# A hybrid decoder layer: the MLP's second product in seven block products as well, in quarters, with more weight sums by DMA and more small sums on GpSimd

## The chip, the cores and the metric

The kernel is one program on one NeuronCore of a Trainium2 chip. The metric is device time in microseconds (us), from one launch; the span is the time from the first to the last instruction in a profiled execution.

## The reference, cut to what matters

One decoder layer on 512 tokens of width 1024: retention and sparse attention in parallel, a merge and an output projection, then the MLP and a gate with per-layer embeddings. All is float32. The part that matters here:

```python
x = x + (g_ret * o_ret + g_nsa * o_nsa) @ w_out[i]
h2 = rms_norm(x, norm_mlp_g[i])
x = x + jnp.square(jax.nn.relu(h2 @ w_mlp_up[i])) @ w_mlp_down[i]      # 1024 -> 4096 -> 1024
x = x + (p[i] @ w_ple_proj[i]) * jax.nn.sigmoid(rms_norm(x, norm_ple_g[i]) @ w_ple_gate[i])
return rms_norm(x, norm_final_g)
```

## The kernel before, in words

Activations lie transposed: partitions are features, the 512 columns are tokens. Float32 accuracy comes from splitting each operand into a high and a low part; a product of a 128x128 weight tile with a block of activations is three matmuls (hi·hi, hi·lo, lo·hi; `mm3`, L264 to L266), summed in PSUM. Weights come by DMA into a ring of three `raw` tiles of 128x1024 (512 KB). Each half of such a tile (128x512) is split by `split_part`: ScalarE copies the high part (L214), VectorE subtracts for the low part (L217). High and low parts have rings of four.

The order of the work is a list of `Item`s that `run` goes through: for each item the splits of its weights, its matmuls, then splits for items ahead (`look`), then the deferred functions, then its `post` (what reads PSUM). Every engine executes its own instructions in the order in which this list issues them.

The MLP's first product (Up, 1024 to 4096) is done in seven block products instead of eight: tokens in two halves of 256, the contraction in two halves, the hidden outputs in pairs of 128. Per pair `UpPair` makes the products m1, m2, p3 to p7, each 4 x 3 matmuls of 256 columns. Their activations (x00, x10, x11 and the sums t1 to t4) are made once, at the end of the out projection, by `combined`, whose sums are on GpSimd (L1390 to L1392). Their weights are blocks of `w_mlp_up` and four sums of blocks, s1 to s4, which are built in DRAM earlier, during the retention heads: 32 plain copies issued from ScalarE and 32 accumulating DMAs issued from GpSimd (`sum_steps`, L360). After the products VectorE and ScalarE add the pieces, VectorE squares (L1489), ScalarE takes the high part (L1490), VectorE the low part (L1491).

The second product (Down, 4096 to 1024) is plain: per output tile 16 x 3 matmuls of 512 columns per half of the hidden width (`down`). The order is Up for the first half of the hidden width, Down for it, Up for the second half, Down for it. Then come the embedding gate (PLE), for which stored products `pp` are loaded during the last Down, the final norm and the output.

## Time and profile before

| | |
|---|---|
| three timed runs | 1250.19, 1251.27, 1254.92 us; median 1251.27 |
| the profiled execution | 1252.07 us, its span 1250.2 us |
| PE busy | 1227.0 us, 98% of the span |
| VectorE (DVE), ScalarE (ACT), GpSimd (POOL) | 67%, 46%, 19% |
| granted TensorE clock | 0.996 of full speed |

The page divides the span among engines and lines; the views behind it give single instructions in order of time, groups, waits and DMA queues. PE at 98% says that almost any time that PE is not spared is not saved; a helper engine's share says little until it is read stage by stage. Lengths of PE instructions are modelled and overlap; what one costs is read from the distance between starts.

### The profile page before, as it was taken

How to read it: one execution, taken by the hardware profiler on the slowest of the kernel's cores; microseconds unless marked ns; L12 is line 12 of the kernel's file. 1: busy time of each engine (PE TensorE's matmuls, PEld its weight loads, DVE VectorE, ACT ScalarE, POOL GpSimd, SP SyncE). 2: the span in 40 equal slices, each digit the busy share in tenths (PEclk: the TensorE clock that was granted, in tenths of full speed). 3: DMA queues.
4: the chain of work that ended last, by engine and by line, in shares of the span. 5: the costliest groups of instructions: out<-in, count | busy, mean ns of one | idle time of the engine just before them, and what ended most of it. 6: DMA issues, size and time to landing. Idle time of an engine off the chain costs nothing.

```text
span 1250.2 us, 18607 instructions
## 1 busy us (share of the span) xinstructions
PE 1227.0 (98%) x6888; PEld 1047.8 (84%) x6888; DVE 835.9 (67%) x1594; ACT 579.1 (46%) x1215; POOL 237.3 (19%) x234
## 2 busy tenths in 40 slices
PE   7999999999999999999999999999999999999996
PEld 6968898998988887788888878889998889988885
DVE  6766764666667478678878863578883348854567
ACT  5753334332333233567877752366552236633333
POOL 0050110111110014256755600012000000000033
PEclk9999999999999999999999999999999999999998
DMA  7545994887685232211110023334552335563221
GB/s 251 193 138 151 251 234 132 218 214 199 173 226 152 68 93 84 68 52 34 35 35 19 34 68 101 103 134 153 186 178 93 99 115 185 179 213 101 90 80 68
DMA packets 64458, 162.55 MB, mean 130 GB/s; under 512 B 6512, under 2 KB 6896, under 8 KB 64368
## 3 DMA queue, kind: packets, MB, share of 16 engines
q1 hardware_dynamic: 46816, 127.54, 30.9%
q0 software_dynamic: 8704, 16.78, 8.0%
q10 hardware_dynamic: 8848, 17.04, 4.1%
q8 instruction: 54, 0.88, 0.3%
q14 instruction: 36, 0.29, 0.1%
HBM read 157.15 MB, written 37.75 MB: 156 GB/s over the span
## 4 chain that ended last, share of the span: by engine, by line
PE 46%; DVE 5%; ACT 1%; issue 1%; DVEq 0%; ACTq 0%
PE ps_s L266 4%; PE ps_s L264 4%; PE ps_s L265 4%; PE ps_d L266 4%; PE ps_d L265 4%; PE ps_d L264 4%; PE ps_v L264 3%; PE ps_v L266 3%; PE ps_v L265 3%; PE ps_t L265 2%; PE ps_t L266 2%; PE ps_t L264 2%; PE ps_t L1127 2%; PE ps_v L1144 1%; PE ps_v L1143 1%; PE ps_s L1052 1%
## 5 line engine op out<-in xcount | busy, mean ns | idle before, releaser
L214 ACT ACTIVATE hi<-raw 128x512 fp32r<-128x512 f32 (+1 forms) x412 | 250.4, 622 | 238.0 <-PE ps_s L265 54.8
L217 DVE TENSOR_TENSOR lo<-raw,hi 128x512 fp32r<-128x512 f32 (+1 forms) x398 | 279.4, 717 | 58.7 <-ACT hi L214 58.4
L264 PE MATMUL ps_d<-h_hi,hi 128*128 128x512 f32 x216 | 89.6, 415 | 0.0
L266 PE MATMUL ps_d<-h_hi,lo 128*128 128x512 f32 x216 | 85.4, 395 | 0.0
L265 PE MATMUL ps_d<-h_lo,hi 128*128 128x512 f32 x216 | 85.3, 395 | 0.0
L1105 POOL TENSOR_TENSOR pr<-pr,rr 128x512 f32<-128x512 f32 x80 | 84.7, 1091 | 0.0
L217 POOL TENSOR_TENSOR lo_fw<-raw_fw,hi_fw 128x512 fp32r<-128x512 f32 x8 | 11.3, 1440 | 347.3 <-ACT hi_fw L214 347.3
L1070 ACT ACTIVATE pr<-ps_s,nm 128x128 f32<-128x128 f32 (+3 forms) x128 | 66.1, 526 | 21.2 <-DVE sc L1064 15.2
L1136 DVE TENSOR_TENSOR ptl<-ps_t,pth 128x512 fp32r<-128x512 f32 x80 | 53.9, 685 | 16.8 <-ACT pth L1131 14.8
L264 PE MATMUL ps_t<-h_hi,hi 128*128 128x512 f32 x160 | 64.1, 401 | 0.0
L266 PE MATMUL ps_t<-h_hi,lo 128*128 128x512 f32 x160 | 63.4, 396 | 0.4 <-DVE lo L217 0.4
L265 PE MATMUL ps_t<-h_lo,hi 128*128 128x512 f32 x160 | 63.3, 395 | 0.0
L1062 DVE TENSOR_REDUCE nm<-ps_s 128x2 f32<-128x256 f32 (+3 forms) x64 | 52.0, 814 | 14.3 <-PE ps_s L1055 14.0
L360 POOL DMA_DIRECT2D sum_s<-in_w_mlp_up_dram x16 | 18.3, 1147 | 222.8 <-DMA sum_s<-in_w_mlp_up_dram 222.8
L1131 ACT ACTIVATE pth<-ps_t 128x512 fp32r<-128x512 f32 x80 | 47.4, 599 | 22.2 <-PE ps_t L1127 18.3
L266 PE MATMUL ps_s<-hh,lo 128*128 128x512 f32 x128 | 50.5, 395 | 0.0
L264 PE MATMUL ps_s<-hh,hi 128*128 128x512 f32 x128 | 50.5, 395 | 0.0
L265 PE MATMUL ps_s<-hl,hi 128*128 128x512 f32 x128 | 50.5, 395 | 0.0
L266 PEld LDWEIGHTS ps_d<-h_hi,lo 128*128 128x128 f32 x216 | 40.6, 188 | 10.0 <-DVE lo L217 0.3
L1127 PEld LDWEIGHTS ps_t<-cst,pr 128*128 128x128 f32 x320 | 39.3, 140 | 10.7 <-issue 1.6
L1127 PE MATMUL ps_t<-cst,pr 128*128 128x128 f32 x320 | 48.0, 273 | 0.0
L264 PEld LDWEIGHTS ps_d<-h_hi,hi 128*128 128x128 f32 x216 | 40.7, 188 | 7.0 <-ACT tanh L433 0.4
(483 smaller groups left out, 3653.4 us busy)
## 6 DMA issues: line engine op xcount, KB each, us to landing
...
```

The source lines that it names most:

```text
L214: act.activation(p.hi[i], p.raw[:, c], AF.Copy)
L217: eng.tensor_tensor(p.lo[i], p.raw[:, c], p.hi[i].bitcast(F32), op=ALU.subtract)
L264: pe.matmul(ps, sh, mh, start=first, stop=False, skip_group_check=again)
L265: pe.matmul(ps, sh, ml, start=False, stop=False, skip_group_check=again)
L266: pe.matmul(ps, sl, mh, start=False, stop=last, skip_group_check=again)
L360: return [lambda d=d, s_=s_, add_=add_: pool.dma_start(d, s_, accum_op=ALU.add, max_dma_last_dim=4 * S) if add_ else act.dma_start(d, s_) ...
L1062: dve.tensor_reduce(self.nm[:, j, :], self.seen(j), axis=AX.XY, op=ALU.max, negate=True)
L1070: act.activation(self.pr[:, j, br, 0 : self.nk].rearrange("p (b j) -> p b j", j=P), self.seen(j)[:, br], AF.Exp, bias=self.nm[:, j, br : b ...
L1105: pool.tensor_tensor(p, p, self.rr[:, :, 1 + br : 2 + br].broadcast_to([P, 4, P]), op=ALU.mult)
L1127: pe.transpose(self.t[i][:, j * P : (j + 1) * P], self.pr[:, j, br, kb * P : (kb + 1) * P], ident)
L1131: act.activation(hi, self.t[i], AF.Copy)
L1136: dve.tensor_tensor(lo, self.t[i], self.pt[i][0].bitcast(F32), op=ALU.subtract)
```

## The change

Down gets the same seven products as Up. The hidden width goes in four quarters of 1024 instead of two halves: Up of a quarter, Down of it, and so on, eight stages of 28 products (`steps_of`, `mlp`). At each change of stage the first product of the new stage is put ahead of the last of the old one. Down's weights are laid out anew and four sums of their blocks are built like Up's: 64 copies and 64 accumulating DMAs instead of 32 and 32. Of these the first halves run in the heads as before; the other 32 copies go out from ScalarE during the attention, the other 32 accumulating DMAs from GpSimd, spread from the merge to the end of the third MLP stage. Up's results are now squared in pieces and combined per quarter into x00 to t4 (tiles `ht`): four small sums per pair on GpSimd, seven high and seven low parts of 256 columns on ScalarE and VectorE. Down's results are multiplied by the norm factor on VectorE and added to x on GpSimd (on VectorE in the last quarter). The low parts of some weights go to GpSimd: 9 of 28 in Up, 10 of 28 in Down. Two more tiles for high and low parts come from another pool, and splits go five ahead. At the end, five of nine loads for PLE are issued later, and the output tiles are others.

```diff
--- before.py
+++ after.py
@@ part_tile
+        if p.first is not None and (p.first + i) % 6 > 3:
+            return P_["ew"].tile([P, c.stop - c.start], F32R, tag=tag, name=tag, bufs=2)
         return wp.tile([P, c.stop - c.start], F32R, tag=tag, name=tag, bufs=4)
@@ run
-                    split(n)
+                    split(n, eng=pool if order[n][1] in order[n][0].other else dve)
...
-                split(j, ahead > 0)
+                split(j, ahead > 0, pool if order[j][1] in order[j][0].other else dve)
@@ sum_steps
+    wb, sums = {}, {}
+    for name in ("w_mlp_up", "w_mlp_down"):
+        wb[name] = a[name].rearrange("(q i) k (j c) -> i j q k c", i=2, j=2)
+        sums[name] = {x: dram.tile([16, P, S], F32, name=f"{x}_{name}") for x in ("s1", "s2", "s3", "s4")}
...
+            copies.append([(t["s1"], w(1, 1)), (t["s3"], w(0, 0)), (t["s2"], w(0, 0)), (t["s4"], w(0, 1))])
+            for l, level in enumerate(([("s1", w(1, 0)), ("s3", w(1, 0))], [("s2", t["s1"])], [("s4", t["s2"])])):
+                adds.setdefault(c + l, []).extend((t[x], src) for x, src in level)
+        return [[lambda x=x: act.dma_start(*x) for x in g] for g in copies], [[lambda x=x: pool.dma_start(*x, accum_op=ALU.add, max_dma_last_dim=4 * S) for x in adds[n]] for n in sorted(adds)]
@@ the list of items
-    folds_ = sum_steps()
+    chunks = [(name, 4 * qt + i) for qt in range(NQ) for name in wb for i in (0, 2)]
+    copies, adds = sum_steps(chunks[:8])
...
+    copies2, adds2 = sum_steps(chunks[8:])
...
+    copies2 = sum(copies2, [])
+    every = len(ops) // (len(copies2) + 2)
     for i, op in enumerate(ops):
+        if i % every == every - 1 and copies2:
+            add(Item(0, copies2.pop(0)))
...
+    adds2 = sum(adds2, [])
+    merge_at = len(items)
@@ class UpPair, now Pair with the subclasses Up (row0, half1, row1) and Down (added)
-            return Item(1.4, go, getattr(self, "after_" + name, None), piece.parts(col, col + S))
+            return Item(1.4, go, getattr(self, "after_" + name), piece.parts(col, col + S), 5)
...
-        def squares(self, i, t):
-            n = 2 * (self.q % 8) + i
-            hi = P_["hid"].tile([P, S], F32R, tag=f"hh{n}", name="hh")
-            lo = P_["hid"].tile([P, S], F32R, tag=f"hl{n}", name="hl")
-            dve.scalar_tensor_tensor(t, t, 0.0, t, op0=ALU.min if i else ALU.max, op1=ALU.mult)
-            act.activation(hi, t, AF.Copy)
-            defer(lambda: dve.tensor_tensor(lo, t, hi.bitcast(F32), op=ALU.subtract))
+        def row0(self):
+            k, r0 = self.q % 4, self.r0
+            d = self.d = P_["ew"].tile([P, H], F32, tag="hd", name="hd", bufs=2)
...
+            dve.scalar_tensor_tensor(r0, r0, 0.0, r0, op0=ALU.max, op1=ALU.mult)
+            pool.tensor_tensor(d, r0[:, :H], r0[:, H:], op=ALU.subtract)
+            taken("x00", k, r0[:, :H], of="ht")
+            defer(lambda: taken("t1", k, d, of="ht"))
+        def half1(self):
+            n = self.r1[:, H:]
+            dve.scalar_tensor_tensor(n, n, 0.0, n, op0=ALU.min, op1=ALU.mult)
+            taken("x11", self.q % 4, n, of="ht")
+        def row1(self):
+            k, d, r0, r1 = self.q % 4, self.d, self.r0, self.r1
+            act.activation(r1[:, :H], self.a, AF.Relu, scale=-1.0)
+            act.activation(r1[:, :H], r1[:, :H], AF.Square)
+            taken("x10", k, r1[:, :H], of="ht")
+            pool.tensor_tensor(d, d, r1[:, H:], op=ALU.add)
+            pool.tensor_tensor(r0[:, H:], r1[:, H:], r0[:, H:], op=ALU.subtract)
+            pool.tensor_tensor(r0[:, :H], d, r1[:, :H], op=ALU.subtract)
+            def rest():
+                taken("t2", k, d, -1.0, "ht")
+                taken("t3", k, r0[:, H:], of="ht")
+                taken("t4", k, r0[:, :H], of="ht")
+            defer(lambda: defer(rest))
...
+        def added(self, n, r, op):
+            dve.tensor_tensor(r, r, T["rb2"], op=ALU.mult)
+            x = T["x1"][n]
+            (pool if self.q < 12 else dve).tensor_tensor(x, x, r, op=op)
+            if self.q // 4 == NQ - 1:
+                defer(lambda: defer(lambda: gained(n, G_PLE, "acc2")))
@@ ups, down -> steps_of, mlp
-        ps_ = [Piece(a["w_mlp_down"][hf, n, c]) for c in range(2)]
-        return dense(("d", "v", "s", "s")[n % 4], ps_, (lambda: [hid[hf, i] for i in range(16)], 16), post, 4)
+        pooled = {(x, i) for x in ("m2", "p3") for i in range(4)} | ({("p7", 3)} if kind is Up else {("m1", 0), ("m1", 1)})
+        return [(qs[i], x, (x, i) in pooled) for x, i in order_]
...
+        for qt in range(NQ):
+            for kind, name in ((Up, "w_mlp_up"), (Down, "w_mlp_down")):
+                more = steps_of(kind, name, qt)
+                flat = flat[:-1] + more[:1] + flat[-1:] + more[1:] if flat else more
...
-    items += u0[:8] + [token_rstd(("acc1",), "n1", "s")] + u0[8:16] + [over_squared()] + u0[16:]
-    items += sum((down(0, n) for n in range(KT)), [])
-    items += ups(1)
-    dn = [down(1, n) for n in range(KT)]
-    items += dn[0] + [Item(0, load_pp)] + sum(dn[1:], [])
+    items += st_[0][:8] + [token_rstd(("acc1",), "n1", "s")] + st_[0][8:14] + [over_squared()] + st_[0][14:] + st_[1] + st_[2]
+    items[merge_at:] = among(items[merge_at:], adds2)
+    items += sum(st_[3:7], [])
...
+    items += [*dn[:4], Item(0, gx_start), Item(0, load_pp), *among(dn[4:], [lambda i=i: one_pp(i) for i in (0, 2, 4, 6)])]
+    late_pp = [lambda i=i: one_pp(i) for i in (1, 3, 5, 7, 8)]
...
-    items += weave(first[:16], turns[:4])
+    items += among(weave(first[:16], turns[:4]), late_pp)
...
-        "w_mlp_down": _tiles(w_mlp_down[0]).reshape(2, 2, KT, P, 1024).transpose(0, 2, 1, 3, 4),
+        "w_mlp_down": _tiles(w_mlp_down[0]).reshape(NQ * KT, P, NQ, 2, P).transpose(0, 1, 3, 2, 4).reshape(NQ * KT, P, D),
```

On VectorE, in the middle of the second Up stage, it stood like this before (`lo` is a weight's low part, `r0` and `r1` are results of a pair, `hl` the low part of the squared result, `ps` is PSUM, `s12` and `s5` saved pieces):

```order
L217 TENSOR_TENSOR lo_9704<-raw_9579,hi_9687 128x512
L217 TENSOR_TENSOR lo_9725<-raw_9623,hi_9709 128x512
L1473 TENSOR_TENSOR r0_9647<-ps_t_9463,s12_9563 128x256
L1489 SCALAR_TENSOR_TENSOR r0_9647<-r0_9647 128x512
L217 TENSOR_TENSOR lo_9747<-raw_9623,hi_9727 128x512
L1491 TENSOR_TENSOR hl_9731<-r0_9647,hh_9730 128x512
L1467 TENSOR_TENSOR r0_9754<-ps_s_9734,s12_9711 128x256
L217 TENSOR_TENSOR lo_9768<-raw_9663,hi_9751 128x512
L1478 TENSOR_TENSOR r1_9772<-ps_d_9546,s5_9480 128x256
L217 TENSOR_TENSOR lo_9786<-raw_9663,hi_9770 128x512
L217 TENSOR_TENSOR lo_9805<-raw_9706,hi_9790 128x512
L1481 COPY r1_9772<-ps_d_9546 128x256
```

After the change, on VectorE at the end of the second Up quarter (`hd` is a pair's difference, `ht` a high or low part for Down):

```order
L1518 SCALAR_TENSOR_TENSOR r0_10531<-r0_10531 128x512
L224 TENSOR_TENSOR lo_10609<-raw_10474,hi_10589 128x512
L1387 TENSOR_TENSOR ht_10179<-r0_10531,ht_10178 128x256
L1387 TENSOR_TENSOR ht_10181<-hd_10593,ht_10180 128x256
L1387 TENSOR_TENSOR ht_10171<-r1_10570,ht_10170 128x256
L1502 TENSOR_TENSOR r1_10642<-ps_v_10459,s5_10395 128x256
L1525 SCALAR_TENSOR_TENSOR r1_10642<-r1_10642 128x256
L224 TENSOR_TENSOR lo_10659<-raw_10524,hi_10638 128x512
L1387 TENSOR_TENSOR ht_10181<-r1_10642,ht_10180 128x256
L1389 SCALAR_TENSOR_TENSOR ht_10175<-hd_10505,ht_10174 128x256
L1387 TENSOR_TENSOR ht_10175<-r0_10414,ht_10174 128x256
L1387 TENSOR_TENSOR ht_10177<-r0_10414,ht_10176 128x256
```

The 512-wide low parts of results are now narrow ones, more of them, and fewer weights' low parts stand among them.

On GpSimd, from the end of the out projection on, the rows before were these, and the last of them is already in PLE (`gf`, `gd` are tiles of `combined`, `lo_fw` a gate weight's low part):

```order
L1392 TENSOR_TENSOR gf2_8408<-gd2_8411,gf_8621 128x256
L1390 TENSOR_TENSOR gd3_8460<-gd3_8460,gf_8687 128x256
L1391 TENSOR_TENSOR gf3_8457<-gf_8687,gf3_8457 128x256
L1392 TENSOR_TENSOR gf3_8457<-gd3_8460,gf_8687 128x256
L217 TENSOR_TENSOR lo_fw_0_0_12363<-raw_fw_0_12289,hi_fw_0_0_12361 128x512
```

After the change, on GpSimd in the first Up quarter (`s1`, `s3` are weight sums in DRAM):

```order
L1533 TENSOR_TENSOR hd_8887<-hd_8887,r1_8944 128x256
L1534 TENSOR_TENSOR r0_8847<-r1_8944,r0_8847 128x256
L1535 TENSOR_TENSOR r0_8847<-hd_8887,r1_8944 128x256
L224 TENSOR_TENSOR lo_9067<-raw_8937,hi_9050 128x512
L1519 TENSOR_TENSOR hd_9099<-r0_9008 128x256
L369 DMA s1_w_mlp_up_80<-in_w_mlp_up_dram 128x2x512
L224 TENSOR_TENSOR lo_9169<-raw_9047,hi_9151 128x512
L369 DMA s3_w_mlp_up_82<-in_w_mlp_up_dram 128x2x512
L224 TENSOR_TENSOR lo_9188<-raw_9047,hi_9171 128x512
L1533 TENSOR_TENSOR hd_9099<-hd_9099,r1_9129 128x256
L1534 TENSOR_TENSOR r0_9008<-r1_9129,r0_9008 128x256
L1535 TENSOR_TENSOR r0_9008<-hd_9099,r1_9129 128x256
```

Weight sums, weights' low parts and the sums of the results share one queue in the MLP, where before there was nothing.

On PE, at the first change from Up to Down, before (`gt` is an input of Up, `hh` and `hl` are inputs of Down):

```order
L264 MATMUL ps_v_9691<-gt_8238,hi_9807 128x256
L265 MATMUL ps_v_9691<-gt_8239,hi_9807 128x256
L266 MATMUL ps_v_9691<-gt_8238,lo_9826 128x256
L264 MATMUL ps_v_9691<-gt_8246,hi_9807 128x256
L265 MATMUL ps_v_9691<-gt_8247,hi_9807 128x256
L266 MATMUL ps_v_9691<-gt_8246,lo_9826 128x256
L264 MATMUL ps_d_9880<-hh_8826,hi_9830 128x512
L265 MATMUL ps_d_9880<-hl_8827,hi_9830 128x512
L266 MATMUL ps_d_9880<-hh_8826,lo_9847 128x512
L264 MATMUL ps_d_9880<-hh_8929,hi_9830 128x512
```

After the change, on PE at the same change of stage:

```order
L271 MATMUL ps_d_9406<-ht_8904,hi_9307 128x256
L272 MATMUL ps_d_9406<-ht_8905,hi_9307 128x256
L273 MATMUL ps_d_9406<-ht_8904,lo_9323 128x256
L271 MATMUL ps_d_9406<-ht_8912,hi_9307 128x256
L272 MATMUL ps_d_9406<-ht_8913,hi_9307 128x256
L273 MATMUL ps_d_9406<-ht_8912,lo_9323 128x256
L271 MATMUL ps_v_9219<-gt_8264,hi_9328 128x256
L272 MATMUL ps_v_9219<-gt_8265,hi_9328 128x256
L273 MATMUL ps_v_9219<-gt_8264,lo_9346 128x256
L271 MATMUL ps_v_9219<-gt_8272,hi_9328 128x256
L272 MATMUL ps_v_9219<-gt_8273,hi_9328 128x256
L273 MATMUL ps_v_9219<-gt_8272,lo_9346 128x256
```

Down's matmuls have 256 columns, and its first product now stands ahead of Up's last one.

## Rows read from the trace of the kernel before

**Rows 1.** The page, busy time: us, share of the span, instructions
```profile
PE 1227.0 (98%) x6888; PEld 1047.8 (84%) x6888; DVE 835.9 (67%) x1594; ACT 579.1 (46%) x1215; POOL 237.3 (19%) x234
```

**Rows 2.** Three stages: length, busy PE, PEld, DVE, ACT, POOL; clock; DMA share
```profile
1020.57:1100.55 79.98, 79.75 (x673) 79.58 (x672) 67.47 (x118) 46.27 (x93) 0.00 (x0) 1.00 0.55 179
1100.55:1190.15 89.60, 89.60 (x387) 72.20 (x386) 41.59 (x65) 28.96 (x49) 0.00 (x0) 1.00 0.40 136
1190.15:1250.20 60.05, 49.39 (x257) 41.19 (x255) 41.13 (x97) 22.77 (x46) 22.09 (x16) 0.94 0.16 61
```

**Rows 3.** Timeline of PE: start, length, instruction, where the product's stages change
```profile
930.96 0.40 PE L264 MATMUL ps_d<-hh,hi 128*128 128x512 f32 x1
1020.57 0.28 PE L264 MATMUL ps_t<-gt,hi 128*128 128x256 f32 x1
1100.55 0.39 PE L264 MATMUL ps_d<-hh,hi 128*128 128x512 f32 x1
1190.15 0.39 PE L264 MATMUL ps_d<-hi,gx 128*128 128x512 f32 x1
```

**Rows 4.** Waits of PE from 847 to 1191: total, times, longest
```profile
PE ps_v L264 <- DVE r L1478: 0.4, 2, 0.2
```

**Rows 5.** Groups of VectorE in the last Up half: busy, mean ns | idle
```profile
L1489 DVE SCALAR_TENSOR_TENSOR r<-r 128x512 f32<-128x512 f32 x15 | 10.4, 692 | 0.5
L1473 DVE TENSOR_TENSOR r<-ps_t,s 128x256 f32<-128x256 f32 x8 | 3.4, 424 | 3.7 <-PE ps_t L266 3.7
```

**Rows 6.** Timeline of VectorE, end of the out projection
```profile
838.09 1.31 DVE L1364 TENSOR_TENSOR gt<-gf,gt 128x256 fp32r<-128x256 f32 x2
839.31 1.23 DVE L1417 TENSOR_TENSOR acc<-acc,sq 128x512 f32<-128x512 f32 x1
840.47 1.22 DVE L217 TENSOR_TENSOR lo<-raw,hi 128x512 fp32r<-128x512 f32 x1
841.61 0.75 DVE L1364 TENSOR_TENSOR gt<-gf,gt 128x256 fp32r<-128x256 f32 x2
842.28 0.68 DVE L1426 TENSOR_TENSOR x<-ps_s,xs 128x512 f32<-128x512 f32 x1
842.88 0.68 DVE L217 TENSOR_TENSOR lo<-raw,hi 128x512 fp32r<-128x512 f32 x1
```

**Rows 7.** Timeline of GpSimd, same place
```profile
832.49 0.74 POOL L1390 TENSOR_TENSOR gd<-gd,gf 128x256 f32<-128x256 f32 x1 [116.70 <-ACT gf L1386]
833.18 0.75 POOL L1391 TENSOR_TENSOR gf<-gf,gf 128x256 f32<-128x256 f32 x1
833.88 1.20 POOL L1392 TENSOR_TENSOR gf<-gd,gf 128x256 f32<-128x256 f32 x1
838.08 1.03 POOL L1390 TENSOR_TENSOR gd<-gd,gf 128x256 f32<-128x256 f32 x1 [3.00 <-ACT gf L1386]
839.07 0.93 POOL L1391 TENSOR_TENSOR gf<-gf,gf 128x256 f32<-128x256 f32 x1
839.96 1.19 POOL L1392 TENSOR_TENSOR gf<-gd,gf 128x256 f32<-128x256 f32 x1
```

**Rows 8.** Groups of GpSimd: busy, mean ns of one
```profile
L360 POOL DMA_DIRECT2D sum_s<-in_w_mlp_up_dram x16 | 18.3, 1147 | 222.8 <-DMA sum_s<-in_w_mlp_up_dram 222.8
L217 POOL TENSOR_TENSOR lo<-raw,hi 128x512 fp32r<-128x512 f32 x14 | 18.1, 1292 | 34.7 <-ACT hi L214 33.9 <-POOL qcat L983 0.9
```

**Rows 9.** The page, DMA queue of GpSimd: packets, MB, share of 16 engines
```profile
q0 software_dynamic: 8704, 16.78, 8.0%
```

**Rows 10.** DMA queues in the last Up half, 1020 to 1100
```profile
q1 hardware_dynamic: 7295, 14.02, 54.0%
```

**Rows 11.** The same columns, in the heads and in the attention
```profile
120.00:180.00 60.00, 60.00 (x396) 54.73 (x395) 42.49 (x99) 19.84 (x36) 11.38 (x10) 1.00 0.97 248
500.00:700.00 200.00, 198.85 (x1111) 165.00 (x1110) 156.38 (x312) 143.53 (x392) 114.22 (x125) 1.00 0.12 41
```

**Rows 12.** ScalarE's issues of the weight copies: duration min/median/max, first and last start
```profile
L360 ACTq DMA_DIRECT2D sum_s<-in_w_mlp_up_dram x32: 559/559/688, 111.1 to 366.5; - x32
```

More of the change, by code (lines that the diff above doesn't have):

```diff
@@ L48, in __init__ @@
         self.raw, self.hi, self.lo = None, {}, {}
+        self.other = ()
+        self.first = None
     def load(self, sp):
@@ L938, in _layer_kernel @@
     items += [sil0, g0[0], b0[1], g0[1], c1[3], g0[2], c0[0], g0[3], c1[4], c0[1], qk0[0], c0[2], qk0[1], c0[3], qk0[2], qk0[3], c0[4]]
-    folds_ = sum_steps()
+    chunks = [(name, 4 * qt + i) for qt in range(NQ) for name in wb for i in (0, 2)]
+    copies, adds = sum_steps(chunks[:8])
+    folds_ = []
+    for g in range(max(len(copies), 1 + len(adds))):
+        folds_ += (copies[g] if g < len(copies) else []) + (adds[g - 1] if 0 < g <= len(adds) else [])
+    copies2, adds2 = sum_steps(chunks[8:])
     def among(its, steps):
@@ new lines, in hid_start, with row0, half1, row1 @@
+    def hid_start():
+        T["ht"] = {(i, k): [P_["hid"].tile([P, S if i < 3 else H], F32R, tag=f"h{x}{i}{k}", name="ht") for x in "hl"] for k in range(4) for i in range(4)}
+    class Down(Pair):
+        of = "ht"
+        def added(self, n, r, op):
[4 more added lines that the diff above has]
+                defer(lambda: defer(lambda: gained(n, G_PLE, "acc2")))
+        def row0(self):
+            self.added(2 * (self.q % 4), self.r0, ALU.add)
+        def half1(self):
+            pass
+        def row1(self):
+            act.activation(self.r1[:, :H], self.a, AF.Copy)
+            self.added(2 * (self.q % 4) + 1, self.r1, ALU.subtract)
@@ new lines, in mlp @@
+    def mlp():
+        flat, ends = [], []
+        for qt in range(NQ):
+            for kind, name in ((Up, "w_mlp_up"), (Down, "w_mlp_down")):
+                more = steps_of(kind, name, qt)
+                flat = flat[:-1] + more[:1] + flat[-1:] + more[1:] if flat else more
+                ends.append(len(flat))
+        out_ = []
+        for i in range(0, len(flat), 2):
+            pc = Piece([pair.w[x] for pair, x, _ in flat[i : i + 2]])
+            pc.first, pc.other = i, {c for c in range(2) if flat[i + c][2]}
+            out_ += [flat[i + c][0].product(flat[i + c][1], pc, c * S) for c in range(2)]
+        return [out_[i:j] for i, j in zip([0] + ends, ends)]
@@ L1532, in mlp_start, with gx_start @@
         open_("hid", bufs=1)
+    def gx_start():
+        T["gx"] = [tuple(P_["xp"].tile([P, S], F32R, tag=f"gt{x}{i % 4}{i // 4}", name="gx") for x in "hl") for i in range(KT)]
     def load_pp():
```

115 lines of the change are left out of this document (54 added, 61 removed).

## The prediction

> **What bounds the kernel now.** First the page's busy times: PE is busy 1227.0 of 1250.2 us [rows 1], so a gain must come from fewer or shorter matmuls, and a loss from whatever makes PE wait. Then the busy times by stage: the last Up half keeps PE busy 79.75 of 79.98 us and the last Down half 89.60 of 89.60; VectorE is busy 67.47 us in that Up half, GpSimd not at all [rows 2]. The starts at the changes of stage give each stage's length to 0.1 us [rows 3]. PE's waits over the whole MLP are tenths of a microsecond, and the telling one is for VectorE's addition L1478, which must have read PSUM before the next product goes into the same bank [rows 4]. So the MLP is bound by PE, with VectorE close behind in Up. All sums are made against the profiled execution (1252.07 us, span 1250.2); the timed median, 1251.27, is 0.8 us below it, and I subtract that at the end.
>
> **The streaming.** Down is twice 384 matmuls of 512 columns: 1020.57 - 930.96 = 89.61 us and 1190.15 - 1100.55 = 89.60 us [rows 3], together 179.21. Afterwards it is 16 pairs x 7 products x 12 = 1344 matmuls of 256 columns. The last Up half is 672 of just these, in 1100.55 - 1020.57 = 79.98 us, so 1344 take 159.96. Saved: 19.25 us. This is less than an eighth of 179 (22.4), since a narrow matmul costs 0.119 us where half a wide one costs 0.117. From here a quarter stage of 336 matmuls is 39.99 us, and Up and Down of a quarter are 79.98.
>
> **VectorE and GpSimd in the quarters.** This is the term I trust least. At the end of the out projection, the only place in the trace where GpSimd's sums of this kind stand beside VectorE's subtractions, each disturbs the other. Alone, a 256-wide GpSimd sum takes 0.70 us (starts 832.49, 833.18, 833.88) [rows 7]; a 512-wide low part takes 1.29 [rows 8]. A VectorE instruction alone occupies 0.60 us for 512 columns (842.28 to 842.88) and 0.335 for 256 (two in 0.67, from 841.61 on) [rows 6]. Side by side, from 838.08 to 841.61, there are three GpSimd sums (2.1 us alone) and four VectorE instructions (0.67 + 0.60 + 0.60 = 1.87 alone): 3.97 us of work take 3.53, a factor of 0.89. The 1.23 and 1.22 us for 512-wide VectorE instructions there, against 0.68 beside no sum, say that each GpSimd instruction in the way costs VectorE 0.55 [rows 6].
>
> The Trainium skill ("SBUF — State Buffer", section "Who interferes with whom") says that a VectorE instruction with two SBUF inputs contends with a GpSimd instruction that reads SBUF, and that the one that issues second fully blocks. The trace agrees in the main, the factor being 0.89 rather than 1; a strict lock is the second rival below.
>
> Counted in the new program order, an Up quarter has on GpSimd 9 low parts and 16 sums: 9 x 1.29 + 16 x 0.70 = 22.8 us. On VectorE the instructions with both inputs in SBUF are 19 wide low parts, 28 narrow ones, 4 wide and 4 narrow squarings: 23 x 0.60 + 32 x 0.335 = 24.5 us. Together 47.3; times 0.89, 42.1 us, against PE's 40.0. Down: 18 x 1.29 = 23.2 on GpSimd (10 low parts, 8 additions to x), 26 x 0.60 = 15.6 on VectorE, together 38.8, times 0.89 34.5. A turn thus needs 76.6 of 79.98 us: enough, but in Up VectorE falls behind by some 2 us, and splits five ahead do not cover all of it, since PE waits for VectorE's reading of PSUM long before the ring of splits runs dry (L1478 again). Bounds for an Up quarter: 0 (Down catches up everything) and 11.3 (the rival below). I take 1.5 for each of four, near the row-based 2.1: +6.0.
>
> **Changes of stage.** The first product of Down needs the last pair's x00: a sum from PSUM 0.42, a squaring 0.69 [rows 5], a narrow copy on ScalarE (0.42 at the most, estimated from the narrow VectorE row) and a subtraction of 0.34, 1.9 us in all. It starts two products after p3 (2 x 1.43 us), and its last quarter of weights comes 1.07 later, so 3.9 us are there. 2.0 us of slack are about what three instructions lose at 0.55 each (1.65). Before, the same kind of wait cost 0.2 us at a time [rows 4]. Between 0 and 2 us each, I take 0.5, the row's end, for four changes from Up to Down: +2.0. From Down to Up nothing is waited for, since `gt` stands ready.
>
> **Weight sums by DMA.** Of the 32 late accumulating DMAs the program order has 12 before the MLP's stages and 20 in the first three. Weights in the last Up half take 54.0% of 80 us for 14.02 MB [rows 10], so 3.08 us per MB, or 1.62 for a tile of 0.524 MB. An accumulating DMA takes 8.0% of 1250.2 us / 32 = 3.13 us of all 16 engines [rows 9]. In three stages 42 x 1.62 + 20 x 3.13 = 130.6 us of transfer meet 120.0 us of PE. In the heads the engines held 0.97 for 60 us while these sums ran [rows 11], so the transfers need 134.6 us: 14.6 too many. Against that, about five tiles of weights lie loaded or split ahead (8.1 us of transfer), and the last sums may land in the fourth stage, for they are read only from the fifth on. Bounds 0 and 14.6; I take 1.5, near the lower end, for PE needs only the 68 us of weights. GpSimd's 20 issues at 1.15 us [rows 8] lie in its own queue: 7 in an Up quarter make 22.8 + 8.1 = 30.9 of 40 us, covered unless its waits for VectorE exceed 9 us.
>
> **Attention and end.** 32 copies are issued from ScalarE during the attention, 0.56 us each [rows 12], while it is busy 143.5 of 200 us and PE 198.85 [rows 11]. Nothing waits behind an issue unless ScalarE is late: 0, at most 3. In PLE (60.05 us, PE busy 49.39 [rows 2]) five loads now come behind four gate weights of 0.524 MB; 3.6 MB at 3.08 us are 11 us, and they are wanted about 11 us after PLE starts. Before, all of it was loaded early. Between 0 and 4, taken +1.0. No reason speaks for a gain here.
>
> Sum: -19.25 + 6.0 + 2.0 + 1.5 + 1.0 = -8.75, so 1252.07 - 8.75 = 1243.3, and 1242.5 against the timed median; rounded, **1243**.
>
> **Rivals.** (1) The helpers hide completely: VectorE catches up in every Down. Then only the changes of stage remain, 1252.07 - 19.25 + 2.0 - 0.8 = 1234. For it: the sums per turn leave 3.4 us. Against: Up alone is over 40.
> (2) VectorE becomes the bound in the four Up quarters, because every GpSimd instruction excludes it for its whole length: 28.5 us of its own work (24.5 and 12 narrow reads of PSUM at 0.335) plus 22.8 make 51.3, 11.3 over PE, in each. Then 1252.07 - 19.25 + 45.2 - 0.8 = 1277, slower. It decides when the loss per GpSimd instruction passes (40.0 + 25.5/4 - 28.5)/25 = 0.72 us, 25.5 being what turns 19.25 of gain into a loss of 6.25. For it: sum by sum the trace shows VectorE stopped. Against: 0.55, not 0.72, and the overlap of 11%. By the skill's strict lock this would be the outcome.
> (3) The transfers bind in the first three stages: their full 14.6 in place of 1.5, so 1243 + 13 = 1256, no change. For it: 0.97 held in the heads leaves little to spare. Against: the tiles ahead, and sums that may be late.
>
> **How the numbers follow.** A measurement of this kernel tells 0.5%, 6.3 us: faster is below 1245.0, slower above 1257.5. The forecast has a chance of 0.40, its own range 1238 to 1250 (0.30 faster, 0.10 within). Rival 1: 0.22, faster. Rival 3: 0.20, of which 0.02 slower. Rival 2: 0.18, of which 0.13 slower and 0.05 within, since the loss may stop between 0.55 and 0.72. Together faster 0.52, same 0.33, slower 0.15. The range runs from rival 1 with its changes of stage free, 1232, to 1260, just past rival 3; what is left out is most of rival 2.
>
> **What would show it.** The profile after should have 672 matmuls of a quarter pair in about 80 us wherever PE is not waiting. The port term is right if PE's waits in Up quarters are for VectorE (its reads of PSUM and low parts) and add up to about 6 us, with wide low parts on VectorE lasting 0.8 to 1.2 us; it is wrong if these last 0.69, or if PE waits as long in Down. The DMA term is shown by a DMA share near 1 in the first three stages and ScalarE waiting for `raw`; if the share stays below 0.9 there, my price of an accumulating DMA was too high. The end is right if PLE stays within 59 to 64 us. The forecast as a whole falls if the first three stages run over 126 us, or if VectorE is busy through whole Up quarters while PE stands.

## The result, and the profile after

The changed kernel takes 1289.27 us (median of four runs, 1287.67 to 1289.91) beside 1251.16 for the kernel before: a ratio of 1.0297, 95% interval 1.0285 to 1.0309. It is 3% slower, outside the predicted range of 1232 to 1260. The profiled execution has a span of 1287.0 us, 36.8 more than before.

The page of the kernel after, busy times [rows 1]:

```profile
PE 1223.1 (95%) x7464; PEld 1074.2 (83%) x7464; DVE 949.0 (74%) x1686; ACT 658.1 (51%) x1439; POOL 480.8 (37%) x430
```

PE is busy for nearly as long as before in a longer span: it stands, and, as will be seen, part of its busy time is at half clock. Where, the eight quarter stages show (kernel after, columns as in [rows 2]; Up and Down in turn; as the first product of a stage is put ahead, a row runs from the second product of its stage to the second of the next, so the first row has 29 products and the eighth 27; the last row is what follows the MLP):

```profile
846.51:907.91 61.40, 50.93 (x365) 49.97 (x364) 53.64 (x82) 33.88 (x79) 34.78 (x34) 0.86 0.74 184
907.91:956.15 48.24, 42.21 (x338) 41.06 (x337) 39.68 (x48) 23.85 (x52) 30.98 (x25) 0.96 0.84 216
956.15:1006.62 50.47, 43.92 (x338) 43.14 (x337) 41.54 (x59) 30.52 (x74) 36.47 (x33) 0.93 0.88 222
1006.62:1049.02 42.40, 39.56 (x339) 39.18 (x338) 35.44 (x47) 23.84 (x50) 26.57 (x19) 1.00 0.62 187
1049.02:1095.47 46.45, 42.41 (x338) 41.61 (x337) 39.89 (x59) 30.14 (x71) 31.78 (x26) 0.96 0.50 159
1095.47:1135.83 40.36, 39.54 (x339) 38.97 (x338) 34.19 (x47) 23.72 (x50) 27.02 (x19) 1.00 0.59 184
1135.83:1181.05 45.22, 41.13 (x339) 40.13 (x338) 39.06 (x58) 28.71 (x67) 30.57 (x25) 1.00 0.52 163
1181.05:1227.26 46.21, 39.31 (x326) 38.01 (x325) 44.67 (x65) 30.24 (x64) 15.61 (x12) 1.00 0.51 166
1227.26:1287.00 59.74, 49.40 (x258) 41.20 (x256) 42.12 (x99) 23.15 (x47) 22.14 (x16) 0.94 0.30 111
```

The MLP takes 380.75 us against 342.65 before (847.54 to 1190.15); it starts 1.0 us earlier, and the end takes 0.3 less. The undisturbed sixth stage, 40.36, confirms the price of a quarter stage. Two things cost: the first three stages, where the late weight sums run, are 61, 48 and 50 us; and Up quarters without them are still 45 to 46. The longest waits of PE from 846 to 1180 (total, times, longest; before, they were 0.9 us in all, with the 0.4 of [rows 4]):

```profile
PE ps_d L271 <- ACT r L1530: 7.8, 4, 2.3
PE ps_d L271 <- DVE r L1502: 7.8, 4, 3.9
PE ps_d L273 <- DVE lo L224: 3.6, 1, 3.6
PE ps_s L272 <- DVE gt L1387: 2.8, 1, 2.8
```

They are for VectorE's and ScalarE's reads of PSUM and for VectorE's low parts. VectorE's groups, kernel after, 850 to 1228:

```profile
L224 DVE TENSOR_TENSOR lo<-raw,hi 128x512 fp32r<-128x512 f32 x147 | 142.9, 979 | 14.3 <-ACT hi L221 14.0
L1387 DVE TENSOR_TENSOR ht<-r,ht 128x256 fp32r<-128x256 f32 x80 | 62.2, 791 | 6.5 <-ACT ht L1385 6.3
```

A wide low part, 0.60 to 0.68 us alone, averages 0.98. The mean hides a few very long instructions. One place in the first stage; the timeline of GpSimd:

```profile
868.75 1.15 POOL L369 DMA_DIRECT2D s_w_mlp_down<-s_w_mlp_down  x1
869.50 1.16 POOL L1533 TENSOR_TENSOR hd<-hd,r 128x256 f32<-128x256 f32 x1
870.21 1.14 POOL L1534 TENSOR_TENSOR r<-r,r 128x256 f32<-128x256 f32 x1
870.90 1.13 POOL L1535 TENSOR_TENSOR r<-hd,r 128x256 f32<-128x256 f32 x1
871.58 1.66 POOL L224 TENSOR_TENSOR lo<-raw,hi 128x512 fp32r<-128x512 f32 x1
```

The timeline of VectorE at the same time:

```profile
869.66 3.61 DVE L320 TENSOR_TENSOR rs_r<-rs_r,rs_q 128x4 f32<-128x4 f32 x1
873.30 0.16 DVE L315 SCALAR_TENSOR_TENSOR rs_y<-rs_r,rs_y 128x4 f32<-128x4 f32 x1
...
873.97 0.68 DVE L224 TENSOR_TENSOR lo<-raw,hi 128x512 fp32r<-128x512 f32 x1
```

And that of PE:

```profile
870.72 0.28 PE L271 MATMUL ps_d<-gt,hi 128*128 128x256 f32 x1
870.83 0.28 PE L272 MATMUL ps_d<-gt,hi 128*128 128x256 f32 x1
874.71 0.58 PE L273 MATMUL ps_d<-gt,lo 128*128 128x256 f32 x1 [3.60 <-DVE lo L224]
875.09 0.41 PE L271 MATMUL ps_d<-gt,hi 128*128 128x256 f32 x1
875.30 0.41 PE L272 MATMUL ps_d<-gt,hi 128*128 128x256 f32 x1
```

GpSimd issues an accumulating DMA and goes on without a gap through four tensor operations, to 873.24. VectorE's 128x4 operation, 0.16 us at this step in the kernel before, starts at 869.66 and ends with that run. The low part behind it is late, PE waits 3.60 us for it, and then its matmuls start 0.21 us apart instead of 0.12, until 880.0: the lower of TensorE's two levels (1.2 and 2.4 GHz), after an idle stretch. The stage's mean granted clock is 0.86.

The DMA queues of SP (q1) and GpSimd (q0), kernel after, 846 to 1000 [rows 10]:

```profile
q1 hardware_dynamic: 12155, 22.12, 43.7%
q0 software_dynamic: 4904, 9.45, 37.1%
```

The late sums take nearly as much of the DMA engines as the weights. ScalarE's waits for weights in these three stages add up to 24.7 us (in e2 below, without late sums, to 4.6). Over the whole span, the page's queues of GpSimd [rows 9] and ScalarE:

```profile
q0 software_dynamic: 17408, 33.56, 15.4%
q10 hardware_dynamic: 17552, 33.82, 8.0%
```

64 accumulating DMAs take 15.4% of 1287 us, 3.10 us each, which is the 3.13 that I had assumed; 64 plain copies of the same size take 1.61 each.

### The profile page after: what moved, and what is told of

It is laid out like the page before. It is cut to its first block, busy times and chain, and to the rows that moved or that the text cites. A ratio compares the mean times of both kernels' runs of the same rounds, so it can differ in the third digit from the quotient of the medians.

```text
span 1287.0 us, 20585 instructions
## 1 busy us (share of the span) xinstructions
PE 1223.1 (95%) x7464; PEld 1074.2 (83%) x7464; DVE 949.0 (74%) x1686; ACT 658.1 (51%) x1439; POOL 480.8 (37%) x430
## 3 DMA queue, kind: packets, MB, share of 16 engines
q0 software_dynamic: 17408, 33.56, 15.4%
## 4 chain that ended last, share of the span: by engine, by line
PE 30%; DVE 12%; issue 5%; DMA 3%; POOL 2%; ACT 2%; SPq 0%; DVEq 0%; ACTq 0%; POOLq 0%
DVE lo L224 3%; PE ps_d L273 3%; PE ps_d L272 3%; PE ps_d L271 3%; DVE ht L1387 2%; PE ps_t L272 2%; PE ps_t L273 2%; PE ps_t L271 2%; PE ps_t L1142 2%; PE ps_s L272 2%; PE ps_s L273 2%; PE ps_s L271 2%; PE ps_v L271 1%; DMA raw<-s_w_mlp_up 1%; PE ps_v L273 1%
## 5 line engine op out<-in xcount | busy, mean ns | idle before, releaser
L221 ACT ACTIVATE hi<-raw 128x512 fp32r<-128x512 f32 (+1 forms) x460 | 281.8, 622 | 192.4 <-PE ps_v L273 46.5
L224 DVE TENSOR_TENSOR lo<-raw,hi 128x512 fp32r<-128x512 f32 (+1 forms) x370 | 305.5, 835 | 45.4 <-ACT hi L221 44.8
L224 POOL TENSOR_TENSOR lo<-raw,hi 128x512 fp32r<-128x512 f32 x90 | 135.5, 1522 | 85.1 <-ACT hi L221 70.5
L1085 ACT ACTIVATE pr<-ps_s,nm 128x128 f32<-128x128 f32 (+3 forms) x128 | 66.1, 526 | 21.4 <-DVE sc L1079 15.4
L1387 DVE TENSOR_TENSOR ht<-r,ht 128x256 fp32r<-128x256 f32 x80 | 62.2, 791 | 6.5 <-ACT ht L1385 6.3
L1151 DVE TENSOR_TENSOR ptl<-ps_t,pth 128x512 fp32r<-128x512 f32 x80 | 54.0, 685 | 16.7 <-ACT pth L1146 14.5
L1385 ACT ACTIVATE ht<-r 128x256 fp32r<-128x256 f32 x80 | 32.0, 413 | 50.4 <-DVE r L1518 31.8
L369 POOL DMA_DIRECT2D s_w_mlp_up<-in_w_mlp_up_dram x16 | 19.2, 1285 | 102.2 <-DMA s_w_mlp_up<-in_w_mlp_up_dram 102.2
L1555 POOL TENSOR_TENSOR x<-x,r 128x512 f32<-128x512 f32 x24 | 39.8, 1657 | 37.2 <-DVE r L1553 27.7
L984 POOL TENSOR_TENSOR nr<-nr,nr 128x512 f32<-128x512 f32 x8 | 11.8, 1472 | 110.1 <-DVE nr L560 110.1
L369 POOL DMA_DIRECT2D s_w_mlp_down<-in_w_mlp_down_dram x16 | 18.7, 1224 | 86.7 <-DMA s_w_mlp_down<-in_w_mlp_down_dram 86.7
```

Of the source, the lines that this page charges most:

```text
L221: act.activation(p.hi[i], p.raw[:, c], AF.Copy)
L224: eng.tensor_tensor(p.lo[i], p.raw[:, c], p.hi[i].bitcast(F32), op=ALU.subtract)
L1085: act.activation(self.pr[:, j, br, 0 : self.nk].rearrange("p (b j) -> p b j", j=P), self.seen(j)[:, br], AF.Exp, bias=self.nm[:, j, br : b ...
L1151: dve.tensor_tensor(lo, self.t[i], self.pt[i][0].bitcast(F32), op=ALU.subtract)
L1387: defer(lambda: dve.tensor_tensor(lo, v, hi.bitcast(F32), op=ALU.subtract))
```

## The experiments

All are variants of the changed kernel; times are medians beside runs of the kernel before on the same chip, with the ratio to it and its 95% interval. "MLP" is the length from the first Up matmul to the last Down one in the profile; the kernel before has 342.65.

**The two suspects apart: e1 to e4.** e1 computes all weight low parts on VectorE; e3 also the sums and the additions to x; e2 issues no late accumulating DMA; e4 is e3 and e2 together.

```diff
-        pooled = {(x, i) for x in ("m2", "p3") for i in range(4)} | ({("p7", 3)} if kind is Up else {("m1", 0), ("m1", 1)})
+        pooled = set()                                                      # e1, e3, e4
-            pool.tensor_tensor(d, d, r1[:, H:], op=ALU.add)
+            dve.tensor_tensor(d, d, r1[:, H:], op=ALU.add)                  # e3, e4: likewise L1519, L1534, L1535, L1555
-    items[merge_at:] = among(items[merge_at:], adds2)                       # e2, e4
```

> The changed kernel (1289.3 us) with the low parts of MLP weights all back on VectorE: GpSimd keeps its sums and its DMA issues. Theory A (GpSimd's instructions shut VectorE out): a wide low part shuts VectorE out for 1.3 to 1.5 us and takes 0.6 on VectorE itself, 19 of them per turn of Up and Down, so some 12 us less per turn of contended time; 1265 to 1275 us. Theory B (the 20 accumulating DMAs in the first three stages are the cause): VectorE only gets 11 us more work per turn; 1285 to 1295 us.

> The changed kernel without the 32 accumulating DMAs from merge to third stage (the copies stay, so the last two quarters use unsummed weights). The first three stages took 160 us where the third and fourth quarter's pattern would take about 140. Theory B: they fall to that pattern, 1264 to 1270 us. Theory A with GpSimd's tensor instructions alone as cause: hardly anything, 1282 to 1289 us.

> No tensor instruction on GpSimd in the eight MLP stages: low parts, sums and additions to x are all on VectorE, which then has 39.3 us of work of its own in an Up quarter of 40.0 and 30 in Down; the accumulating DMAs stay. Theory A: each wait behind GpSimd goes, only a nearly full VectorE is left; 1250 to 1262 us. Theory B: the first three stages stay long, 1270 to 1285 us.

> Both: no tensor instruction on GpSimd in the MLP and no late accumulating DMAs (the last two quarters use unsummed weights). If A and B together are the whole loss, PE streams as in the Up of the kernel before: 1252.1 - 19.3 plus some waits for a VectorE at 98% in Up, 1236 to 1246 us. If it stays above 1255, a third cause (the clock, the order of the products, the loads at the end) is open.

Measured: e1 1271.75 (1.0170, 1.0155 to 1.0185), e2 1269.28 (1.0149, 1.0132 to 1.0166), e3 1273.23 (1.0186, 1.0162 to 1.0209), e4 1248.59 (0.9985, 0.9976 to 0.9995). Late sums cost 20.0 us (after - e2) or 24.6 (e3 - e4), GpSimd's tensor work 16.0 (after - e3) or 20.7 (e2 - e4), all of it with the low parts (after - e1: 17.5). Without both the change gains 2.5 us, not the 19 of its streaming, and less than I expected. An Up quarter of e4, columns as in [rows 2]:

```profile
1019.80:1061.86 42.06, 40.36 (x338) 39.96 (x337) 38.29 (x84) 27.96 (x67) 0.00 (x0) 1.00 0.53 176
```

The same quarter of e2, without late transfers too:

```profile
1028.50:1074.90 46.40, 42.38 (x338) 41.58 (x337) 39.71 (x59) 30.22 (x71) 31.71 (x26) 0.96 0.50 160
```

GpSimd took 25 of VectorE's 84 instructions, and VectorE is busy 1.4 us longer. What it gave away (9 x 0.69 + 16 x 0.42 = 12.9 us, by e4's durations) it lost again: the durations of the 59 that it kept add up to 43.5 us, against 30.6 at e4's means, so they are 12.9 us longer, 0.52 us for each GpSimd instruction.

**Bytes or issues: e5, e6.** e5 is e3 with late sums of 32 of 512 columns: the same issues, 1/16 of the bytes. e6 is e4 with two plain copies from ScalarE in the place of each late sum.

```diff
-    adds2 = sum(adds2, [])
+    adds2 = sum(sum_steps(chunks[8:], 32)[1], [])                           # e5: 32 columns
+    items[merge_at:] = among(items[merge_at:], plain)                       # e6: 32 x two act.dma_start, 0.5 MB each
```

> e3 (no tensor instruction on GpSimd in the MLP) with each of the 32 late accumulating DMAs cut to 32 of its 512 columns: the same issues on GpSimd, a sixteenth of the bytes (the last two quarters then use weights that are not fully summed). If the transfers fill the DMA engines, the 24.6 us that separate e3 (1273.2) from e4 (1248.6) go: 1248 to 1253 us. If the issues on GpSimd are what costs (they shut VectorE out for 1.1 us each), they stay: 1265 to 1273 us.

> e4 (no tensor instruction on GpSimd, no late accumulating DMAs) with two plain copies of 0.5 MB from DRAM to DRAM issued from ScalarE where each accumulating DMA stood; nobody reads their results. The same time of DMA engines (2 x 1.6 us against 3.1), no GpSimd, and spread by ScalarE's queue over all three stages. If the load on the DMA engines is the cause: 1258 to 1272 us, with ScalarE waiting for raw weights. If it is GpSimd's queue or the accumulating form: 1249 to 1253 us.

Measured: e5 1248.78 (0.9984, 0.9973 to 0.9994), e4's time; e6 1267.26 (1.0124, 1.0099 to 1.0149), 18.7 more. Where GpSimd has no tensor work, load on the DMA engines is the cost and the issues are free: e3 and e5 have the same issues and differ by 24.5 us, and over the first three stages ScalarE waits for weights 32.2 us in e3, 25.8 in e6 and 3.3 in e5. The plain copies of e6 also take some 8 us of ScalarE's own time per stage to issue; what that costs was not tried apart. I took the load for the whole answer at first.

**GpSimd's work without its results: e7, e12.** Both are e4 plus additions on a tile that nobody uses, about as many and as wide as the changed kernel's (e12: 160 beside 164), each batch paced by a 4-column read: in e7 of result tiles, in e12 of tiles that ScalarE wrote.

```diff
+    def idle(t, *widths):
+        g = T["gf"]
+        pool.tensor_tensor(g[:, D - 4 :], t[:, :4], t[:, :4], op=ALU.add)
+        for w in widths:
+            pool.tensor_tensor(g[:, S : S + w], g[:, :w], g[:, :w], op=ALU.add)
```

> e4 with additions on GpSimd on a tile that nobody waits for: per Up quarter 9 of 512 columns and 16 of 256, per Down 18 of 512, each small group started by a 4-column read of a result just made. Same occupation of GpSimd as in the changed kernel, but no result is ever waited for. If the loss comes from GpSimd's instructions shutting VectorE out, e4's 1248.6 becomes 1262 to 1275 us and wide low parts on VectorE last over 0.8 us on average. If it came from waiting for GpSimd's late results: 1248 to 1252 us.

> As e4 (second half's weight sums left out of the computation), and GpSimd does additions of the count and width of the changed kernel's (9 of 512 and 16 of 256 columns in an Up quarter, 18 of 512 in a Down quarter) on a tile that no other engine reads or writes; to keep pace it reads 4 columns, 12 times a quarter, of tiles that ScalarE wrote and that nobody writes again for two products. Theory (GpSimd's accesses hold up VectorE's, whoever wants the result): wide low parts on VectorE go from 683 ns in e4 to 850 ns or more, and the time is e4's plus 8 to 21 us, 1257 to 1270 us. Rival (what costs is that GpSimd's results come late, 1.57 us against 0.68 us for a low part, in the chain that TensorE waits for): VectorE's 683 ns may grow, but the time stays within 4 us of e4, 1248 to 1253 us.

Measured: e7 1348.13 (1.0769, 1.0750 to 1.0789), e12 1314.95 (1.0507, 1.0491 to 1.0524). Both are beyond what any theory gave. e7 is flawed: VectorE overwrites the tiles that GpSimd reads, and waited for it. e12 has no such wait, and its MLP is 406.1 us against e4's 339.7. VectorE's wide low parts in e4, 850 to 1228:

```profile
L224 DVE TENSOR_TENSOR lo<-raw,hi 128x512 fp32r<-128x512 f32 x230 | 154.1, 690 | 0.8
```

And in e12:

```profile
L224 DVE TENSOR_TENSOR lo<-raw,hi 128x512 fp32r<-128x512 f32 x211 | 184.8, 897 | 0.4
```

So GpSimd's accesses hold VectorE up whoever wants the result; late results are not needed for a loss. In the changed kernel VectorE is relieved of 43 instructions per turn in exchange (25 in Up, 18 in Down), which fits its losing 16 to 21 us and not 66; e12's 96 paced reads are in the 66 too.

**Late sums elsewhere: e8, e9, e11.** e8 is e3 with the late sums spread over the attention, one step behind their copies. e9 issues the copies in retention heads 5 to 7, 24 sums in the attention, 8 in the merge. e11 is e9's order with all of the changed kernel's GpSimd work.

```diff
-    items[merge_at:] = among(items[merge_at:], adds2)
+        folds2 += (copies2[g] if g < len(copies2) else []) + (adds2[g - 1] if 0 < g <= len(adds2) else [])   # e8
+        if h > 4:
+            its = among(its, copies2[len(copies2) * (h - 5) // (NH - 5) : len(copies2) * (h - 4) // (NH - 5)])  # e9, e11
+    copies2, adds2 = adds2[:24], adds2[24:]
```

> A version with the whole computation: no tensor instruction on GpSimd in the MLP, and the 32 late accumulating DMAs among the attention, each group behind its copies, where the DMA engines were used to 0.12 before. If the two costs are all, it comes out at e4's 1248.6 plus little: 1247 to 1254 us. If GpSimd's queue in the attention is held up by waits for the copies, 1255 to 1265 us.

> The whole computation. As e3 (no addition, subtraction or low part of the MLP on GpSimd), but the second half's plain copies of weight slices are issued during the last three retention heads (320 to 460 us, where the DMA share of e4 was 0.49), 24 of its 32 accumulating transfers during the attention, and the last 8 behind the merge and output products, all before the MLP. Theory (what the late accumulating transfers cost is the DMA engines' time, taken from the weight loads of a stage that reloads a piece every 2.9 us): the MLP is as in e4, eight quarter stages of 47, 40 to 42 and 44 us, and since the copies are long done when an accumulating transfer is issued, GpSimd is not held in the attention as in e8: 1248 to 1252 us. Rival (any 32 accumulating transfers, wherever they are, cost some time of GpSimd, 5 us in e8): 1254 to 1257 us. Second rival (the copies at a DMA share of 0.85 delay the retention heads' weights): the MLP starts more than 4 us later than in e4.

> The whole computation. The changed kernel with all its GpSimd work in the MLP kept; only the late copies and accumulating transfers are placed as in e9. Theory (the two costs add: 16.0 to 20.7 us for GpSimd's tensor work, 20.0 to 24.6 us for the late transfers): e9 plus 16 to 21 us, 1265 to 1272 us, with the Up quarters longer than e9's by 2 to 5 us and the Down quarters nearly as e9's. Rival (GpSimd's work hurts only while the weights are late): within 5 us of e9.

Measured: e8 1256.00 (1.0037, 1.0024 to 1.0049), e9 1264.80 (1.0109, 1.0094 to 1.0124), e11 1288.06 (1.0283, 1.0261 to 1.0305). The MLP came out as expected: 339.3, 339.0 and 361.7, so GpSimd's work costs 22.7 with no transfer near it, and its inner Up quarters stay at 45 to 46. But the MLP starts at 854.0 in e8, 5 later than in e4, and at 864.1 in e9, 15 later. All my theories missed the cause: the copies in e9's heads delay nothing (PE is busy 140.00 of 140 us from 320 to 460, at a DMA share of 0.82). VectorE in e9's attention:

```profile
650.55 7.58 DVE L1102 TENSOR_TENSOR sc<-sc,cm 128x128 f32<-128x128 f32 x1
```

GpSimd at the same time:

```profile
649.71 1.17 POOL L369 DMA_DIRECT2D s_w_mlp_up<-in_w_mlp_up_dram  x1
650.47 7.47 POOL L1125 TENSOR_TENSOR pr<-pr,rr 128x512 f32<-128x512 f32 x7
657.48 1.58 POOL L369 DMA_DIRECT2D s_w_mlp_up<-in_w_mlp_up_dram  x1
```

An instruction that takes 0.38 us at this place in e4 takes 7.58: as at 869 in the changed kernel, an issue with a run of tensor operations behind it, and VectorE stands until the run is over. A second, of 6.11 us, is at 708.04. Of the 15 us, 12 are lost by PE in the attention (busy 304.8 us from 460 to 780, in e4 316.7).

**Issues among tensor work: e13, e14.** The counterparts of e5 and e6 with GpSimd's work kept: e13 has the late sums of 32 columns, e14 plain copies from ScalarE in their place (same edits, on the changed kernel).

> The changed kernel with all its GpSimd work and all its late accumulating transfers issued from the same places, but each of 32 columns in place of 512 (1/16 of the bytes; the second half's weights are then not fully summed). First theory (an issue on GpSimd, followed by a run of tensor operations, holds VectorE until the run ends; this is a large part of the 20 us that the late transfers cost beside GpSimd's work): VectorE instructions of 2.5 us and more stay in the first three quarter stages, and the time stays 8 us or more above e2 (1269.3 us): 1277 to 1287 us. Second theory (what costs is the transfers' share of the DMA engines): within 4 us of e2, 1266 to 1273 us.

> The changed kernel with all its GpSimd tensor work, but in place of each late accumulating transfer two plain copies of the same size between places in DRAM that nobody reads, issued by ScalarE: about the same time of the DMA engines and no issue on GpSimd (the second half's weight sums are left out of the computation). First theory (issues hold VectorE): no VectorE instruction beyond 2 us in the MLP, and 1270 to 1280 us. Second theory (DMA share): as in e6 over e4 (18.7 us) on top of e2, 1284 to 1291 us.

Measured: e13 1283.70 (1.0260, 1.0246 to 1.0274), e14 1282.44 (1.0250, 1.0233 to 1.0267), so 14.4 and 13.2 us above e2. First stage of e13, columns as above (e2: 53.60 us, DMA share 0.46):

```profile
846.57:905.62 59.05, 47.84 (x365) 47.04 (x364) 54.45 (x81) 34.25 (x80) 35.76 (x35) 0.91 0.47 138
```

First stage of e14:

```profile
848.50:905.88 57.38, 47.67 (x365) 45.35 (x364) 48.82 (x83) 34.81 (x82) 32.99 (x29) 0.97 0.80 262
```

Neither theory holds alone. With hardly any bytes the issues cost most of the 20 us, through VectorE (54 of 59 us busy); with no issues the load costs nearly as much, through late weights: over the first three stages ScalarE waits for them 24.7 us in e14, 12.7 in e13 and 4.6 in e2. (ScalarE's own time for e14's copies, 7 to 8 us per stage, is in its 13.2 too.) Together they cost 20, not 27.6, so their waits overlap: taken away last, the bytes are worth 5.6 us (after - e13), the issues 6.8 (after - e14). In the MLPs of the changed kernel and e13 there are 9 and 10 single VectorE instructions of 2.05 to 7.28 us, each behind an issue with tensor operations directly after it; in those of e2, e11 and e14, without issues, none is above 1.84, and in those of e3 and e5, with issues and no tensor operations of the MLP, none above 1.24.

**A place where they are free: e15, e16.** Both do the whole computation with e3's VectorE. e15: third quarter's sums in retention heads 6 and 7, the last quarter's from the merge to the third MLP stage, each issue paced by a 4-column read. e16: all sums but the last Down's by the end of the heads, 24 copies before the first head, the rest in the merge and output products.

```diff
-    copies, adds = sum_steps(chunks[:8])
+    copies, adds = (sum(x, []) for x in sum_steps(chunks[:14]))             # e16
+    copies2, adds2 = sum_steps(chunks[14:])
+    items[first:] = among(items[first:], copies[:24])
```

> The whole computation, no tensor operation of the MLP on GpSimd (as e3). The weight sums of the third quarter are copied in retention heads 4 and 5 and added in heads 6 and 7, where GpSimd was busy for 7 of 140 us; those of the last quarter are copied in the attention and added from the merge to the third quarter stage of the MLP, each issue paced by a 4-column read of a tile that TensorE's results have just made. Both theories together (transfers cost where the DMA engines are full, issues where GpSimd has a run of tensor operations behind them; here is neither): MLP as in e4 (339 to 342 us), attention as in e4, 1248 to 1252 us, against 1273 for the same work in e3. Rival (an accumulating transfer costs some 0.2 to 0.8 us of the path wherever it stands): 1255 to 1273 us.

> The whole computation, no tensor operation of the MLP on GpSimd (as e3). The weight sums of all quarters but the last Down are made by the end of the retention heads (the first 24 plain copies are issued before the first head, where the DMA share was 0.46), those of the last Down are copied in the attention and added during the merge and output products, paced as in e15; none is issued in the attention or meant for the MLP. Theory (transfers cost only where the DMA engines are full or GpSimd has a run of tensor operations behind their issue): MLP as in e4, 338 to 342 us from a start at 847 to 850, and 1247 to 1252 us. Rival (more transfers in the heads make weights late there): the MLP starts later than 853 and the time is 1254 us or more. Second rival (the last 8 transfers slip into the first MLP stage): the first quarter stage is above 50 us.

Measured: e15 1258.88 (1.0061, 1.0047 to 1.0075): attention as in e4, but with 10 of the last 16 transfers issued in the MLP its first stage is 7.3 us longer than e4's and the next two 1.5 and 1.9. e16 1252.57 (1.0014, 1.0006 to 1.0023), just outside what I expected: the loss is gone, but it is only level with the kernel before. A stretch of its heads, and a Down and the Up behind it in its MLP:

```profile
120.00:220.00 100.00, 100.00 (x561) 86.54 (x560) 59.70 (x125) 34.97 (x63) 27.58 (x24) 1.00 1.09 274
...
979.07:1062.41 83.34, 80.53 (x675) 79.75 (x673) 73.42 (x149) 52.91 (x121) 0.00 (x0) 1.00 0.56 178
```

A DMA share of 1.09 costs the heads nothing; 0.8 to 0.9 cost the MLP, whose weights alone take 0.54 [rows 10]. Down and Up of a quarter are 83.3 us, against (79.98 + 89.60) / 2 = 84.8 before [rows 2]: 1.5 us of the 4.8 that streaming should give.

**VectorE relieved by ScalarE: e10.** e9 with one of two squarings per row pair on ScalarE.

```diff
-            dve.scalar_tensor_tensor(n, n, 0.0, n, op0=ALU.min, op1=ALU.mult)
+            act.activation(n, n, AF.Relu, scale=-1.0)
+            act.activation(n, n, AF.Square)
```

> The whole computation. As e9, and one of the two squarings of each Up row pair (256 wide, 0.69 us on VectorE) moves to ScalarE as a Relu and a Square. Theory (with nothing on GpSimd, VectorE at about 98% of an Up quarter is what makes it 42.1 us and not 40.4): VectorE gets 4 x 0.69 = 2.8 us back in each Up quarter, and the Up quarters go to 40.4 to 41 us: 4 to 6 us less than e9, 1243 to 1247 us. Rival (the 2 us are a chain of dependent steps at each change of stage, through VectorE and ScalarE): within 1.5 us of e9, or slower, since the two ScalarE steps are longer than the one on VectorE.

Measured: 1273.04 (1.0174, 1.0155 to 1.0193), slower than e9; Up quarters go from 42.1 to 43.0 us, though VectorE falls from 38.3 to 36.8 busy. So these quarters are not bound by VectorE's load but by a chain. A wait of ScalarE from 846 to 1180 that is new in e10:

```profile
ACT r L1530 <- DVE r L1507: 12.4, 16, 1.1
```

PE's waits for ScalarE's read of PSUM in e10, 1030 to 1180 (in e9 1.7 and 0.6 us for the two banks):

```profile
PE ps_d L271 <- ACT r L1536: 2.5, 2, 1.3
...
PE ps_v L271 <- ACT r L1536: 1.5, 2, 0.8
```

ScalarE works in order; what it waits for from VectorE delays the read of PSUM behind it. No version tried beats the kernel before by more than 0.16% (e5; e4 0.15%), and both leave weight sums out.

## Why the prediction was wrong

The profiled spans differ by 36.8 us. By MLP lengths: streaming -19.25 (taken from the prediction); what e4's MLP has above that, 339.7 - (342.65 - 19.25) = +16.3; GpSimd's tensor work, e2 over e4, 359.0 - 339.7 = +19.3; late sums, after over e2, 380.75 - 359.0 = +21.7; start and end -1.3. The sum is 36.8. Taken away in the other order (e3's MLP is 362.2) GpSimd's work is 18.6 and the late sums 22.5; by the times above the orders differ by some 4 us.

- **Streaming: right.** Down quarters without waits are 40.2 to 40.4 us, predicted 39.99.
- **Weight sums by DMA: +1.5 predicted, +21.7 measured; this step failed most.** It failed twice. "PE needs only the 68 us of weights" judged the stage by its total, but each piece has its own deadline: the share was 0.74 to 0.88, below the 0.9 that I had set as a sign, and yet the load cost 13 us with no issue on GpSimd (e14) and 24.5 with no tensor work there (e3 over e5). The first is the size of rival 3, which I gave 0.20. And that GpSimd's 20 issues "lie in its own queue" and are "covered" was wrong in kind: behind an issue VectorE is held for all of GpSimd's run (e13, 14 us), which no row of before showed, as no tensor operations followed an issue closely there.
- **VectorE and GpSimd: +6.0 predicted, +19.3 measured.** The price was right: 0.55 us per GpSimd instruction from [rows 6], 0.52 in e2. What failed is what I did with it. I compared sums of busy time with PE's 40 us (42.1, so 1.5 to 2.1 late); VectorE is busy 39.7 of 46.4 us, so it had room, but its products come late where ScalarE and PE wait in order. Rival 2 needed more than 0.72 us per instruction to turn the sign; at 0.52 the term already took all that streaming gives. By the Trainium skill ("SBUF — State Buffer", section "Who interferes with whom") the instruction that issues first keeps the port for its whole length. The trace agrees for single instructions (low parts up to 1.81 us in e11); but 7.58 us behind an issue is a run of seven GpSimd instructions, and here the measurement decides.
- **Changes of stage: +2.0 predicted, +16.3 measured with everything else away.** The bound of 2.0 us each was met in three Up quarters (42.1 us in e4) with no GpSimd work at all, but by another wait than the one in the sum. I priced what Down's first product needs, the last pair's x00; PE's waits in e4's MLP are for VectorE (L1502) and ScalarE (L1530) to read PSUM before the next product goes into the same bank:

```profile
PE ps_v L271 <- DVE r L1502: 8.4, 8, 2.8
PE ps_d L271 <- ACT r L1530: 3.3, 4, 0.8
PE ps_d L271 <- DVE r L1502: 1.6, 2, 1.4
```

All of them are 15.8 us. At each change from Up to Down PE waits 0.8 us for ScalarE and 0.8 for VectorE, which are the 2.1 us of an inner Up quarter; and 0.7 at each change from Down to Up, where the prediction had "nothing is waited for". The rest are places that the sum did not have. At 1.43 us per product the first stage (47.4 us, 29 products) is 6.0 too long, of which 3.4 were there before, and the last Down (44.4, 27 products) 5.8, with two waits of 1.4 and 2.8 us for L1502. e10 shows that the chain through ScalarE lengthens Up quarters; why VectorE reads late in the first and the last stage no run takes apart, and that stays open (in the first, VectorE is busy 46.4 of 47.4 us).
- **Clock: not in the prediction.** From PE's timeline, matmuls that start 0.20 to 0.27 us after the one before lose 14.5 us in the changed kernel's MLP and 2.8 in e4's. So some 12 us of the loss, inside the terms above, are matmuls at the lower level. Each fall of the granted clock in this MLP came during a wait of 2 to 4 us or soon after it, though not every such wait brought one.
- **Attention and end: small, as predicted.** Predicted +1.0, measured -1.3; the MLP's start alone lies between 846.5 and 848.9 us in the runs that leave heads and attention as they are in the changed kernel, so the sign says nothing.
